# When ScalarE's evacuations, Silu and the stores of the gated product are issued in a hybrid block's gate/up loop

## The chip, the core and the metric

The kernel runs on one core of a Trainium2 chip. The core has a matrix engine (TensorE, PE in the profile), three engines that work on tiles in on-chip memory (VectorE = DVE, ScalarE = ACT, GpSimd = POOL) and a queue engine that starts transfers (SyncE = SP). ScalarE and GpSimd start transfers too. The metric is device microseconds of one execution, as a median of several runs.

## The reference

One transformer block in float32: a sequence of 512 tokens, width 2048. The input projection feeds a state space mixer (SSD) and an attention with three branches; their results go through the output projection. Then follows a gated feed-forward part and a final norm. What the change touches is the feed-forward part:

```python
    v = rmsnorm(h, ffn_norm_w[l])
    h = h + (jax.nn.silu(v @ w_gate[l]) * (v @ w_up[l])) @ w_down[l]
return rmsnorm(h, final_norm_w)
```

Its width is 5632, so the gate and up products are [512 x 2048] by [2048 x 5632] each, and the down product is [512 x 5632] by [5632 x 2048].

## The kernel before

**Numbers.** Every float32 operand is split into a high part, rounded to the matrix engine's fp32r format, and a low part, the rest. A product is made of three matmuls (high by high, high by low, low by high). High parts are written by ScalarE (`a_hi`, line 122), low parts by VectorE (`lo`, line 125, and `neg_lo`, line 128).

**Strassen-like products.** In the feed-forward part a 2 x 2 block product is made with seven products M1 to M7 (names on line 44) of sums of blocks. For the activations these sums are made once, into seven tiles: V0, two tiles in U, and four tiles T. For the weights, four blocks and two sums per pair of column blocks are kept: "11", "12", "22", "S1", "S3" (and "21" in the down part); S1 and S3 come from two transfers, of which the second adds into the first. `quad` (line 1290) says which block each product takes, and which sums have to be made by VectorE just before (for M6 and M3).

**Gate/up.** The 5632 columns are 22 pairs `u` of 256. A pair has two sides, 0 for gate and 1 for up. For pairs 1 to 20 side 0 runs all seven products in the order `SEQ` (M1 M5 M6 M2 M7 M3 M4, line 46), and then side 1 does. The first pair (0) and the last (21) run their sides side by side (`both_sides`, line 1484, with an explicit order). One product is one *step* (`run_step`, line 1156): 8 groups of two matmuls, one with 512 columns (high weights by high and low activations together), one with 256. Each side has three PSUM banks (`BANK`, line 59): M1, M6, M7 and M4 add up in bank X, M5 and M3 in bank R, and M2 is added in bank W to a copy of M1. Adding up in the bank saves additions later, but each partial sum has to be read out before the next product adds to it.

**What follows a product.** `gu_after` (line 1363) reads each bank out after its product: M1 is copied by ScalarE from bank X to bank W (line 1379), M6 is copied from X (line 1381), M2 from W (line 1389), M5 from R (1395), M7 and M3 are added by VectorE, M4 is copied (1411) and then VectorE adds halves of all four buffers into the side's result. After M4 of the gate side VectorE multiplies by the row scale (`rr`), ScalarE applies Silu in two instructions (1417 and 1418), and VectorE multiplies by the row scale again (`times_r`, 1426). After M4 of the up side VectorE multiplies both sides, and `g_forms` (1430) splits the result and four sums of its quarters into high and low parts, and stores them in DRAM (`g_d`, line 1450, issued on ScalarE's queue).

**Order of issue.** From `run_rest` on, the program order of each engine's queue is the order in which the Python code issues. Each step first issues the weight forms of later steps (`prep`: the high part of the step three ahead, with the sums, and the low part of the step two ahead), then its matmuls, and after each of its 8 matmul groups a *tick* (`Sched`, line 71). A generator that yields n goes on n ticks later, so 8 ticks are one step. After the matmuls the step issues its read-out. An engine does its instructions in its own program order, so what is issued first can hold up what stands behind it.

**Down.** 35 visits (`VISITS`, line 23) each multiply some rows of weight blocks for one of 8 column blocks `j`. The hidden activations come back from DRAM into a ring of 7 slots (`GRING`), which are the seven activation tiles of the gate/up part: a slot can be loaded when the last pair's product that reads the tile is done. `feed` (line 1529) is called before each step and issues these loads on ScalarE's queue, in two halves: products 0 to 3 of the list (M1, M2, M3, M6) in the first half, and M5, M7, M4 in the second. In a visit the order is `SEQ_D` (M1 M2 M6 M3 M7 M4 M5), so that the fifth product is the first to read a second half. `place` (line 1068) picks room for a weight block on its way in: for the down part in a zone of 38 rows, first at multiples of six, then anywhere. `advance` (1084) issues a load as soon as there is room, on SyncE's queue, and an adding transfer on GpSimd's.

**Waits between transfers.** Transfers issued by SyncE and ScalarE share a rotation of eight completion semaphores, so that a new one can wait for the one eight before it.

Of the kernel before, what the change touches and what calls it, by code (L numbers as in the profile page):

```python
# [10 lines left out]
AF = mybir.ActivationFunctionType  # L11
# [6 lines left out]
NP = NFF // 2  # L18
# [7 lines left out]
GRING = 7  # L26
# [17 lines left out]
M1, M2, M3, M4, M5, M6, M7 = range(1, 8)  # L44
# [10 lines left out]
NA, NZ, NZ2 = 76, 48, 38  # L55

NR, NE = 48, 8
# [55 lines left out]
def body(ctx, tc, xT, w_in, w_out, w_gate, w_up, w_down, w1k, w1v, cols, rows, kst, out):  # L113
    nc = tc.nc
    act, dve, pool, pe = nc.scalar, nc.vector, nc.gpsimd, nc.tensor
    sch = Sched()
# [4 lines left out]
    def a_hi(dst, src, scale=1.0):  # L121
        act.activation(dst, src, AF.Copy, scale=scale)  # L122
# [7 lines left out]
    def mul(eng, o, a, b):  # L130
        eng.tensor_tensor(o, a, b, ALU.mult)  # L131

    def add(eng, o, a, b):
        eng.tensor_tensor(o, a, b, ALU.add)  # L134
# [825 lines left out]
    P2 = {}  # L960
# [96 lines left out]
    def take(n, *found):  # L1057
        found = [x for x in found if x]
        if not found:
            return None  # L1060
        _, at, z = min(found, key=lambda x: x[0])
        z.busy[at:at + n] = [True] * n
        return z, at


    fz, az, tz, hz, ez = Zone("Z", NZ), Zone("A", 8), Zone("A2", 6), Zone("R", NR), Zone("E", NE)

    def place(b):
        n = b.n
        if b.down:  # L1070
            return take(n, fz.find(n, NZ2, range(0, NZ2 - 5, 6)) or fz.find(n, NZ2), ez.find(n) if "E2" in P2 and n <= NE else None,
                        tz.find(n) if "A2" in P2 and n <= 6 else None)
        return take(n, fz.find(n), az.find(n))

# [288 lines left out]
    def gu_after(u, side, got):  # L1363
        both = u in (0, NP - 1)

        def after(pr):
            def ev(p):
                wv = P2["A"][:, 12:28, :].rearrange("p (b a) t -> p b (a t)", b=4)
                if both:
                    wv = wv[:, 2 * side:2 * side + 2]  # L1370
                u2, m5 = wv[:, 0 if both else 1, :], wv[:, 1 if both else 3, :]
                ct = P2["CT"].rearrange("p (s c a) t -> p s c (a t)", s=2, c=2)
                c = ct[:, side].rearrange("p a t -> p (a t)")
                g = ct[:, 0].rearrange("p a t -> p (a t)")
                c4 = c.rearrange("p (a t) -> p a t", a=4)
                if pr == M1:
                    if u:
                        got["W"] = bank()
                    act.activation(got["W"] if u else m5, p, AF.Copy)  # L1379
                elif pr == M6:  # L1380
                    act.activation(u2, p, AF.Copy)
                elif pr == M2:
                    if u == 0:
                        add(dve, m5, p, m5)
                        add(dve, c4[:, 0], m5[:, lo_h], m5[:, hi_h])
                    elif both:
                        fold(c4[:, 0], p)
                    else:
                        act.activation(wv[:, 0, :], p, AF.Copy)
                elif pr == M5:  # L1390
                    if u == 0:
                        dve.tensor_tensor(m5, p, m5, ALU.subtract)
                        add(dve, u2, p, u2)
                    else:
                        act.activation(m5, p, AF.Copy)
                elif pr == M7:
                    add(dve, m5, p, m5)
                    if u == 0:
                        add(dve, c4[:, 1:4:2], wv[:, :, lo_h], wv[:, :, hi_h])
                elif pr == M3:  # L1400
                    if u == 0:
                        act.activation(m5, p, AF.Copy)
                    else:
                        add(dve, u2, p, u2)
                        if both:
                            add(dve, c4[:, 1:4:2], wv[:, :, lo_h], wv[:, :, hi_h])
                elif pr == M4:
                    if both:
                        fold(c4[:, 2], p)
                    else:  # L1410
                        act.activation(wv[:, 2, :], p, AF.Copy)
                        add(dve, c4, wv[:, :, lo_h], wv[:, :, hi_h])
                    if side == 0:
                        rr = rrow[:, None, :].to_broadcast([128, 2, 512])
                        c2 = ct[:, 0]
                        mul(dve, c2, c2, rr)
                        act.activation(g[:, 0:512], g[:, 0:512], AF.Silu)
                        act.activation(g[:, 512:1024], g[:, 512:1024], AF.Silu, scale=-1.0)
                        sch.add(times_r(c2, rr))
                    else:  # L1420
                        mul(dve, c, c, g)
                        sch.add(g_forms(u))
            return ev
        return after

    def times_r(c2, rr):
        yield 8
        mul(dve, c2, c2, rr)

    def g_forms(u):  # L1430

        ct = P2["CT"].rearrange("p (s c a) t -> p s c (a t)", s=2, c=2)
        g = ct[:, 1]
        tg = ct[:, 0].rearrange("p a t -> p (a t)").rearrange("p (a t) -> p a t", a=4)
        sg = P2["ST"][:, 0:14, :].bitcast(F32R).rearrange("p (v s) t -> p v s t", s=2)
        a_hi(sg[:, 0, 0, :], g[:, 0, lo_h])
        a_hi(sg[:, 1:3, 0, :], g[:, 1, :].rearrange("p (a t) -> p a t", a=2), scale=-1.0)
        gq = g.rearrange("p c (a t) -> p (c a) t", a=2)
        dve.tensor_tensor(tg[:, 1, :], gq[:, 1, :], gq[:, 0, :], ALU.subtract)
        add(dve, tg[:, 2, :], gq[:, 1, :], gq[:, 3, :])  # L1440
        add(dve, tg[:, 0, :], tg[:, 1, :], gq[:, 3, :])
        dve.tensor_tensor(tg[:, 3, :], tg[:, 0, :], gq[:, 2, :], ALU.subtract)
        yield 4
        lo(dve, sg[:, 0, 1, :], g[:, 0, lo_h], sg[:, 0, 0, :])
        neg_lo(sg[:, 1:3, 1, :], g[:, 1, :].rearrange("p (a t) -> p a t", a=2), sg[:, 1:3, 0, :])
        a_hi(sg[:, 3:7, 0, :], tg)
        yield 4
        lo(dve, sg[:, 3:7, 1, :], tg, sg[:, 3:7, 0, :])
        yield 6
        nc.scalar.dma_start(g_d[u].rearrange("v p n -> p v n"), f(sg).rearrange("p v s t -> p v (s t)"))  # L1450
        sch.flags.add(("g", u))
# [32 lines left out]
    def both_sides(u, order, seq):  # L1484
        loads.extend(qs[u, int(a[0])][a[1:]] for a in order.split())
        bk = {i: gu_banks() for i in range(2)}
        af = {i: gu_after(u, i, bk[i][0]) for i in range(2)}
        for n, (side, p) in enumerate(seq):
            ev = af[side](p)
            if u == 0 and n in (1, 4):  # L1490
                ev = step_r3(ev)
            q = qs[u, side]
            b, sums = q["form"][p]
            if u == 0 and p in (M3, M6):
                sums = [(q["11"], q["S1"]), (q["12"], q["11"])] if p == M3 else ()
            if u and n == 0:
                before = lambda: P2.update(spare=P2["ST"][:, 14:16, :])
            else:
                before = start_ff(n) if u == 0 and n < 7 else None
            s = Step(b, v_rhs(p), bk[side][1](p), after=ev, before=before, sums=sums,  # L1500
                     wide=True)
            if (u, side) == (NP - 1, 1):
                n = V_SLOT.index(V_OF[p]) - GRING
                done[n, 0] = done[n, 1] = s.i

    done = {}
    both_sides(0, "011 111 0S1 012 112 1S1 0S3 022 1S3 122", [(i, p) for p in (M1, M2, M3) for i in range(2)] +
               [(0, M6), (0, M5), (0, M7), (1, M6), (0, M4), (1, M5), (1, M7), (1, M4)])
    for u in range(1, NP - 1):
        for side in range(2):  # L1510
            add_loads(qs[u, side])
# [15 lines left out]
    later = {}  # L1527

    def feed(i):

        for half, r in ((0, slice(0, 4)), (1, slice(4, 7))):
            n = nxt["ring", half]
            if n < NP and max(done.get((n - GRING, half), i), later.get(n, 0)) + 3 <= i:
                if n == NP - 1:
                    sch.run_until(("g", n))
                G[n] = P2["slot"][n % GRING]
                nc.scalar.dma_start(f(G[n][:, r]).rearrange("p v s t -> p v (s t)"),
                                    g_d[n, r].rearrange("v p n -> p v n"))
                nxt["ring", half] += 1
        if "H0" not in P2 and len(G) > 0 and not any(az.busy):  # L1540
            load_h(0)
            P2["H0"] = True
# [352 lines left out]
```

## Time and profile before

| | |
|---|---|
| median of 3 runs | 2302.05 us (2302.01 to 2304.55) |
| the profiled execution's own time | 2301.49 us |
| its span, first to last instruction | 2299.5 us |
| mean granted TensorE clock | 0.982 |
| busy TensorE / VectorE / ScalarE / GpSimd | 95% / 79% / 51% / 18% |
| mean transfer rate | 181 GB/s |
| input projection to output projection | 0 to 893 us |
| first gate/up pair | 893 to 944 us |
| pairs 1 to 20 | 944 to 1764 us |
| last pair | 1764 to 1807 us |
| down part and end | 1807 to 2299 us |

The profile is of one execution. In its timelines a row has the start, the length, the engine, the line, the operation, the tiles (written <- read), the shapes and how many such instructions were merged; in square brackets stands how long the engine had been idle before, and what ended that. In a list of waits stand the total, the number and the longest. A line such as 122 belongs to a helper, so that the tiles say which use it is.

### The profile page before, as it was taken

Reading aid. Unit: us, or ns where it says so; the run is one execution under the profiler, and the core shown is the slowest. Engines: PE = TensorE matmul, PEld = TensorE weight load, DVE = VectorE, ACT = ScalarE, POOL = GpSimd, SP = SyncE. Lnnn points to the kernel's source line nnn. Section 1 sums busy time; section 2 is a strip of 40 time slices with the busy share of each in tenths; the row PEclk is TensorE's granted clock in tenths of the full one; section 3 lists DMA queues with packets and bytes.
Section 4 is the critical chain, followed back from the end, with each engine's and each line's share of the span. In section 5 each row is a group of like instructions: output and inputs, shape, how many; then the busy total and the mean of one; then the engine's idle time right before and its main releaser. Section 6 shows DMA issues by size and latency. Waiting matters only on the chain. (4 is left out here: it accounts for less than half of the span.)

```text
span 2299.5 us, 34934 instructions
## 1 busy us (share of the span) xinstructions
PE 2184.9 (95%) x12904; PEld 1916.1 (83%) x12904; DVE 1824.0 (79%) x2858; ACT 1183.4 (51%) x1961; POOL 425.2 (18%) x433
## 2 busy tenths in 40 slices
PE   7999999999989899999999999999999898999996
PEld 5888888888868687888888888888888798999996
DVE  6699766688888667888788887888878787888897
ACT  4564456566766444555555555555555343333453
POOL 1011334323232133000001000000000121121222
PEclk8999999999989899999999999999999999999998
DMA  5222343122324265878777787787877969696974
GB/s 174 92 70 74 130 139 103 64 92 73 127 70 138 90 214 146 230 206 249 212 231 224 209 248 211 234 222 209 247 212 216 315 223 298 171 301 165 303 193 132
DMA packets 168554, 417.16 MB, mean 181 GB/s; under 512 B 16592, under 2 KB 23520, under 8 KB 168384
## 3 DMA queue, kind: packets, MB, share of 16 engines
q1 hardware_dynamic: 99776, 252.24, 32.4%
q0 software_dynamic: 25888, 76.72, 17.1%
q10 hardware_dynamic: 42720, 85.99, 11.0%
q8 instruction: 101, 1.65, 0.3%
q14 instruction: 69, 0.57, 0.1%
HBM read 353.80 MB, written 57.41 MB: 179 GB/s over the span
## 5 line engine op out<-in xcount | busy, mean ns | idle before, releaser
L122 ACT ACTIVATE R<-Z 128x1024 fp32r<-128x1024 f32 (+4 forms) x459 | 420.6, 931 | 448.5 <-DVE Z L134 316.5
L125 DVE TENSOR_TENSOR R<-Z,R 128x1024 fp32r<-128x1024 f32 (+4 forms) x365 | 387.2, 1067 | 42.2 <-ACT R L122 25.6
L232 PE MATMUL ps_g<-u,whi 128*128 128x512 f32 x720 | 285.5, 397 | 0.2 <-DVE h L131 0.2
L234 PE MATMUL ps_g<-u,wlo 128*128 128x512 f32 x720 | 284.0, 394 | 0.0
L233 PE MATMUL ps_g<-u,whi 128*128 128x512 f32 x720 | 283.4, 394 | 0.0
L1168 PE MATMUL ps_s<-u,R 128*128 128x512 f32 (+1 forms) x1152 | 251.4, 347 | 2.3 <-DVE R L125 2.3
L1168 PEld LDWEIGHTS ps_s<-u,R 128*128 128x128 f32 x1152 | 187.8, 188 | 29.7 <-DVE R L125 2.8
L125 DVE TENSOR_TENSOR wlo<-wraw,whi 128x512 fp32r<-128x512 f32 x196 | 151.4, 775 | 64.9 <-ACT whi L122 64.3
L122 ACT ACTIVATE whi<-wraw 128x512 fp32r<-128x512 f32 x196 | 122.6, 626 | 131.3 <-PE ps_g L233 84.7
L234 PEld LDWEIGHTS ps_g<-u,wlo 128*128 128x128 f32 x720 | 135.3, 188 | 26.9
L232 PEld LDWEIGHTS ps_g<-u,whi 128*128 128x128 f32 x720 | 135.4, 188 | 25.9 <-DVE h L131 0.5
L233 PEld LDWEIGHTS ps_g<-u,whi 128*128 128x128 f32 x720 | 135.5, 188 | 25.3
L1168 PE MATMUL ps_s<-T,R 128*128 128x512 f32 (+1 forms) x552 | 127.3, 357 | 27.2 <-ACT ps_t L1379 27.2
L1168 PE MATMUL ps_t<-u,R 128*128 128x512 f32 x592 | 134.0, 352 | 2.1 <-DVE A L134 2.1
L134 DVE TENSOR_TENSOR A<-ps_g,A 128x512 f32<-128x512 f32 (+1 forms) x114 | 74.0, 656 | 77.2 <-PE ps_g L1168 38.5
L1168 PE MATMUL ps_g<-u,R 128*128 128x512 f32 (+1 forms) x600 | 131.9, 348 | 1.4 <-DVE R L125 1.4
L1168 PEld LDWEIGHTS ps_s<-T,R 128*128 128x128 f32 x552 | 88.3, 188 | 52.1 <-ACT ps_t L1379 39.7
L1168 PE MATMUL ps_g<-T,R 128*128 128x512 f32 (+1 forms) x584 | 127.1, 349 | 1.3 <-DVE R L125 1.3
L122 ACT ACTIVATE R<-A 128x1024 fp32r<-128x1024 f32 (+3 forms) x78 | 73.3, 939 | 97.8 <-DVE A L134 60.6
L1168 PE MATMUL ps_s<-V,R 128*128 128x512 f32 (+1 forms) x568 | 122.8, 347 | 0.0
L125 DVE TENSOR_TENSOR E<-Z,R 128x1024 fp32r<-128x1024 f32 x94 | 114.7, 1221 | 9.6 <-PE ps_t L1168 5.6
L1172 PE MATMUL ps_g<-u,R 128*128 128x256 f32 (+1 forms) x353 | 114.9, 326 | 7.6 <-ACT R L122 7.6
(486 smaller groups left out, 5728.3 us busy)
## 6 DMA issues: line engine op xcount, KB each, us to landing
Z<-in_w_gate SPq DMA_DIRECT2D x96, 512.0 KB, 4.7
Z<-in_w_up SPq DMA_DIRECT2D x93, 512.0 KB, 6.2
wraw<-in_w_in SPq DMA_DIRECT2D x164, 256.0 KB, 2.6
g_d<-A ACTq DMA_DIRECT2D x22, 1792.0 KB, 7.5
Z<-in_w_gate POOLq DMA_DIRECT2D x39, 512.0 KB, 7.8
Z<-in_w_up POOLq DMA_DIRECT2D x37, 512.0 KB, 5.7
Z<-in_w_down SPq DMA_DIRECT2D x58, 320.0 KB, 5.8
Z<-in_w_down SPq DMA_DIRECT2D x39, 384.0 KB, 3.9
```

The costliest lines, as they stand in the source:

```text
L122: act.activation(dst, src, AF.Copy, scale=scale)
L125: eng.tensor_tensor(dst, src, f(hi), ALU.subtract)
L134: eng.tensor_tensor(o, a, b, ALU.add)
L232: pe.matmul(p, hi_t[i][:, j, :], ah, start=(k == 0), stop=False)
L233: pe.matmul(p, hi_t[i][:, j, :], al, start=False, stop=False)
L234: pe.matmul(p, lo_t[i][:, j, :], ah, start=False, stop=(k == u.nk - 1))
L1168: pe.matmul(o, w, x, start=start, stop=(k == n - 1 and o is q), skip_group_check=not fresh[0])
L1172: pe.matmul(q, h[:, k, :], ah, start=(k == 0), stop=False)
```

## The change

Five things change.

1. In `place`, a down weight block is put in the best free room anywhere in the zone; it is not first tried at multiples of six.
2. In the first pair, M1 is copied to the buffer `u2` in place of `m5`. M2 is no longer read out by itself; it stays in its bank until M6 is done, and is then added to M1. The order of the second half of the pair alternates the sides to the end: M6 M6 M5 M5 M7 M7 M4 M4. In the list of weight loads, the up side's S3 comes ahead of the gate side's 22.
3. Silu is no longer issued right behind M4 of the gate side. A generator issues it 10 ticks later in pairs 1 to 20 (in the second matmul group of the second step after M4), at once in the first and last pair; the second multiplication by the row scale follows 6 ticks behind it (before, 8 ticks behind M4). A flag makes M4 of the up side wait in the issuing program until that multiplication is issued.
4. `g_forms` starts 10 ticks later. With its further waits of 4, 4 and 6 ticks, the store to `g_d` is issued at tick 24 behind M4 of the up side; before, it was tick 14.
5. In `feed`, several loads can be issued in one step. The first halves of slots 0 and 1 wait for the product behind the one that frees them, and the second halves of slots 0 to 4 wait until the slot of the last first half is free.

```diff
@@ place
-            return take(n, fz.find(n, NZ2, range(0, NZ2 - 5, 6)) or fz.find(n, NZ2), ez.find(n) if "E2" in P2 and n <= NE else None,
+            return take(n, fz.find(n, NZ2), ez.find(n) if "E2" in P2 and n <= NE else None,
@@ gu_after
                 if pr == M1:
                     if u:
                         got["W"] = bank()
-                    act.activation(got["W"] if u else m5, p, AF.Copy)
+                    act.activation(got["W"] if u else u2, p, AF.Copy)
                 elif pr == M6:
+                    if u == 0:
+                        add(dve, u2, got["W"], u2)
+                        add(dve, c4[:, 0], u2[:, lo_h], u2[:, hi_h])
                     act.activation(u2, p, AF.Copy)
                 elif pr == M2:
-                    if u == 0:
-                        add(dve, m5, p, m5)
-                        add(dve, c4[:, 0], m5[:, lo_h], m5[:, hi_h])
-                    elif both:
+                    if u and both:
                         fold(c4[:, 0], p)
-                    else:
+                    elif u:
                         act.activation(wv[:, 0, :], p, AF.Copy)
...
                         mul(dve, c2, c2, rr)
-                        act.activation(g[:, 0:512], g[:, 0:512], AF.Silu)
-                        act.activation(g[:, 512:1024], g[:, 512:1024], AF.Silu, scale=-1.0)
-                        sch.add(times_r(c2, rr))
+                        sch.add(silu(u, g, c2, rr, 0 if both else 10))
                     else:
+                        sch.run_until(("r", u))
                         mul(dve, c, c, g)
                         sch.add(g_forms(u))
...
-    def times_r(c2, rr):
-        yield 8
+    def silu(u, g, c2, rr, n):
+        yield n
+        act.activation(g[:, 0:512], g[:, 0:512], AF.Silu)
+        act.activation(g[:, 512:1024], g[:, 512:1024], AF.Silu, scale=-1.0)
+        yield 6
         mul(dve, c2, c2, rr)
+        sch.flags.add(("r", u))
@@ g_forms
+        yield 10
         a_hi(sg[:, 0, 0, :], g[:, 0, lo_h])
@@ the first pair
-    both_sides(0, "011 111 0S1 012 112 1S1 0S3 022 1S3 122", [(i, p) for p in (M1, M2, M3) for i in range(2)] +
-               [(0, M6), (0, M5), (0, M7), (1, M6), (0, M4), (1, M5), (1, M7), (1, M4)])
+    both_sides(0, "011 111 0S1 012 112 1S1 0S3 1S3 022 122", [(i, p) for p in (M1, M2, M3) for i in range(2)] +
+               [(i, p) for p in (M6, M5, M7, M4) for i in range(2)])
@@ feed
-            n = nxt["ring", half]
-            if n < NP and max(done.get((n - GRING, half), i), later.get(n, 0)) + 3 <= i:
+            while nxt["ring", half] < NP:
+                n = nxt["ring", half]
+                at = max(done.get((n - GRING, half), i), later.get(n, 0))
+                if n < 2 and half == 0:
+                    at = done.get((n + 1 - GRING, 0), i)
+                if n < 5 and half == 1:
+                    at = done.get((4 - GRING, 0), i) + n // 2
+                if at + 3 > i:
+                    break
```

## The prediction

> **What bounds the kernel now.** I read the page first, then TensorE's waits, then windows, then the timelines of TensorE, ScalarE and VectorE around one pair of gate/up columns.
>
> ```profile
> PE 2184.9 (95%) x12904; PEld 1916.1 (83%) x12904; DVE 1824.0 (79%) x2858; ACT 1183.4 (51%) x1961; POOL 425.2 (18%) x433
> ...
> PE ps_s L1168 <- ACT ps_t L1379: 27.2, 39, 1.1
> ...
> PE ps_s L1172 <- DMA u<-g_d: 7.2, 2, 5.4
> PE ps_s L1172 <- ACT R L122: 5.8, 2, 5.0
> ```
>
> TensorE is busy 95% of the span, so only its gaps can be won. The largest group is 39 waits for line 1379, the copy of product M1 out of PSUM. Two waits are for the ring of hidden activations (u<-g_d), at the step from gate/up to down.
>
> ```profile
> 781.00:784.40 3.40, 1.86 (x14) 1.54 (x14) 3.40 (x11) 2.67 (x8) 0.49 (x1) 1.00 0.20 77
> ...
> 941.50:944.90 3.40, 3.40 (x12) 2.82 (x12) 1.55 (x2) 1.34 (x2) 0.85 (x1) 0.50 0.29 45
> 944.90:1763.60 818.70, 791.48 (x4480) 683.87 (x4479) 667.07 (x679) 443.07 (x580) 69.09 (x80) 1.00 0.80 225
> 1772.90:1818.10 45.20, 35.41 (x198) 30.58 (x199) 32.22 (x40) 20.81 (x31) 4.47 (x4) 0.93 1.02 363
> 1811.90:1818.70 6.80, 3.07 (x14) 3.07 (x15) 6.38 (x12) 4.14 (x7) 0.74 (x1) 0.50 1.02 373
> ```
>
> In each row stand the window, its length, busy PE, PEld, DVE, ACT, POOL, the granted clock, the DMA share and GB/s. The steady pairs (third row) run at full clock although TensorE pauses in each; VectorE is 81% busy there. The granted clock is halved in two of these windows, 941.5 and 1811.9.
>
> Now the steady pair. A step is one product, 16 matmuls; a side's order is M1 M5 M6 M2 M7 M3 M4.
>
> ```profile
> 964.14 2.94 PE L1168 MATMUL ps_s<-V,R 128*128 128x512 f32 x16
> 970.26 3.04 PE L1168 MATMUL ps_s<-T,R 128*128 128x512 f32 x16 [0.38 <-ACT ps_t L1379]
> 973.14 2.95 PE L1168 MATMUL ps_t<-u,R 128*128 128x512 f32 x16
> 981.52 2.94 PE L1168 MATMUL ps_s<-u,R 128*128 128x512 f32 x16
> 987.08 2.98 PE L1168 MATMUL ps_g<-T,R 128*128 128x512 f32 x16
> 991.12 3.09 PE L1168 MATMUL ps_s<-T,R 128*128 128x512 f32 x16 [1.06 <-ACT ps_t L1379]
> ```
>
> From 981.52 (M4, up side) to 987.08 (M5, next gate side) are two steps, 5.56 us: a step without a wait is 2.78. From 964.14 (M1, up side) to 970.26 (M6) are two steps in 6.12, 0.56 too long, and the following step has 2.88, 0.10 too long: gate to up costs 0.66. At the other boundary M5 to M6 takes 4.04, 1.26 too long, and about 0.15 after it: up to the next gate costs 1.41. With 20 boundaries of the first kind and 19 of the second that is 13.2 + 26.8 = 40.0 us of excess, the size of 39 waits plus their restarts. The cause stands on ScalarE:
>
> ```profile
> 967.61 0.64 ACT L1417 ACTIVATE A<-A 128x512 f32<-128x512 f32 x1 [2.55 <-DVE A L131]
> ...
> 969.63 0.58 ACT L1379 ACTIVATE ps_t<-ps_s 128x512 f32<-128x512 f32 x1
> ...
> 987.75 0.94 ACT L122 ACTIVATE A<-A 128x256 fp32r<-128x256 f32 x2 [2.55 <-DVE A L131]
> 988.60 1.05 ACT L122 ACTIVATE R<-Z 128x1024 fp32r<-128x1024 f32 x1
> ...
> 990.50 0.57 ACT L1379 ACTIVATE ps_t<-ps_s 128x512 f32<-128x512 f32 x1
> ...
> 992.55 0.37 ACTq L1450 DMA_DIRECT2D g_d<-A  x1
> ...
> 995.92 0.58 ACT L1381 ACTIVATE A<-ps_s 128x512 f32<-128x512 f32 x1
> ```
>
> The Silu (967.61) and the result splits (987.75) are each 2.55 us late for VectorE's product, and the M1 copy stands behind them in ScalarE's program order. M6 adds into the bank that the copy reads, so it waits.
>
> **The change part by part.** (a) Silu behind the next M1's copy. Its two instructions now follow ten ticks, in the second matmul group of M5. M1 ends at 964.14 + 2.78 = 966.92, and the copy can end 0.6 later, near 967.6, 2 us before M6 (969.70). Then come one weight copy (1.05) and the two Silu (0.6 each): about 969.9. Behind Silu now stand the M5 copy, whose bank is next written by M3, three steps on, and, on VectorE, the second product with the scale (1.22), moved to the end of M5: 971.2. It has behind it the sum for M3's weights (1.15: 972.4), this the weight copy of ScalarE (1.05: 973.4), and this the evacuation of M6 (0.58: 974.1), which M7 needs at 964.14 + 4 x 2.78 = 975.26. About 1.2 us are left, so this boundary loses its wait: 20 x 0.66 = **13.2 us gained**. If the spare were used up the wait would only move; gaining nothing is the low bound.
>
> (b) Result splits ten ticks later. This also frees the M1 copy, but what the splits start has to be followed to its end: their sums and low parts on VectorE, then at tick 24 the store of g_d, issued **on ScalarE's queue** (L1450). Before, tick 14 put that issue ahead of the M5 copy, where lateness was harmless. Tick 24 is the last tick of M6, so it now stands directly ahead of the M6 copy (L1381), and M7 adds into that bank. The issue waits for the last low part on VectorE. That chain, from the second boundary's rows:
>
> ```profile
> 986.49 1.22 DVE L131 TENSOR_TENSOR A<-A 128x1024 f32<-128x1024 f32 x1
> 987.75 0.43 DVE L1439 TENSOR_TENSOR A<-A 128x256 f32<-128x256 f32 x1
> ...
> 989.22 1.22 DVE L125 TENSOR_TENSOR R<-Z,R 128x1024 fp32r<-128x1024 f32 x1
> 990.36 0.42 DVE L125 TENSOR_TENSOR A<-A 128x256 fp32r<-128x256 f32 x1
> ...
> 991.30 1.22 DVE L125 TENSOR_TENSOR A<-A 128x1024 fp32r<-128x1024 f32 x1
> ...
> 993.68 1.23 DVE L134 TENSOR_TENSOR Z<-Z 128x1024 f32<-128x1024 f32 x1
> 994.83 1.22 DVE L125 TENSOR_TENSOR R<-A,R 128x1024 fp32r<-128x1024 f32 x1
> ```
>
> Start to start, a low part of weights takes 1.14 (989.22 to 990.36), the four sums 1.47 (987.75 to 989.22), the two small low parts 0.94 (990.36 to 991.30), a weight sum 1.15 (993.68 to 994.83). In the new order VectorE does after the product (done 987.71): low part of M6's weights, of M2's, the four sums, the two small low parts, the sum for M3, the low part of M7's weights, then the last low part. 987.75 + 1.14 + 1.14 + 1.47 + 0.94 + 1.15 + 1.14 = 994.73, and the last one ends 1.22 later at 995.95. The issue takes 0.37, the M6 copy 0.58, with some 0.12 between them for semaphores (an estimate: M1's copy ends at 991.07 and M6 starts at 991.12, 0.05 for one hand-over): M7 could start near 997.0. Undisturbed it would start at 987.08 + 3 x 2.78 = 995.42. So the wait goes from M6 to M7 and is 1.6 us, with 0.13 for the restart 1.73, against 1.41 before: 19 x 0.32 = **6.1 us lost**. Bounds: no wait at all, 26.8 gained; VectorE 0.3 later, 11.8 lost. I take the walk, since each of its durations is a row of this stage.
>
> (c) First pair side by side to its end; M1's copy into the other half of the buffer.
>
> ```profile
> 898.35 0.60 ACT L1379 ACTIVATE A<-ps_s 128x512 f32<-128x512 f32 x1 [2.17 <-POOL A L1249]
> ...
> 904.82 2.83 PE L1168 MATMUL ps_s<-u,R 128*128 128x256 f32 x15 [2.33 <-DVE R L125]
> ...
> 939.37 0.68 DVE L134 TENSOR_TENSOR A<-ps_t,A 128x512 f32<-128x512 f32 x1
> ...
> 940.20 0.47 PE L1168 MATMUL ps_t<-u,R 128*128 128x512 f32 x1 [2.06 <-DVE A L134]
> ```
>
> The first M1 copy waited 2.17 us for a GpSimd operation that reads the buffer it writes; the half it now writes is last read earlier. The VectorE chain behind it, which ends in the wait of 2.33, moves up: 2.2 us (bounds 0 and 4). The wait at 940.20 is M4 of the up side right behind M7 of the same side, with the bank still read at 939.37; side by side, M4 of the gate side (2.78 us) lies between, and the add ends 1.9 us after M7. That saves 2.06, and 1.7 for the 3.4 us of half clock in the window at 941.5. Against it, pair 0's store meets pair 1 as in (b), with a shorter VectorE chain (0.42 in place of 1.22): about 0.8. Sum **5.2**, bounds 0 and 7. The moved M2 evacuation and the loads' order cost nothing: each of these steps brings VectorE one low part (1.14) and at most 1.2 us of evacuation in 2.78 us of matmuls; without that cover the M2 evacuations (two of 1.1) would come back.
>
> (d) Ring loads: first halves early, second halves held back, and a looser placement of down weights.
>
> ```profile
> 1774.04 2.86 PE L1168 MATMUL ps_g<-T,R 128*128 128x256 f32 x15 [1.30 <-DVE R L125]
> ...
> 1792.51 2.84 PE L1168 MATMUL ps_g<-u,R 128*128 128x256 f32 x15 [1.41 <-DVE R L125]
> ...
> 1809.62 0.39 PE L1172 MATMUL ps_s<-u,R 128*128 128x256 f32 x1 [1.85 <-DMA u<-g_d]
> ...
> 1815.63 0.58 PE L1172 MATMUL ps_s<-u,R 128*128 128x256 f32 x1 [5.40 <-DMA u<-g_d]
> ...
> 1823.83 0.29 PE L1172 MATMUL ps_g<-u,R 128*128 128x256 f32 x1
> ...
> 1824.55 0.28 PE L1172 MATMUL ps_s<-V,R 128*128 128x256 f32 x1
> ```
>
> These four gaps make 10.0 us, and the 6.8 us at half clock add 3.4: 13.4 is the most to win. But the bytes stay: 45.2 us at 363 GB/s and a full DMA share. The second boundary's M1 starts at 987.08 - 2.78 = 984.30, and 19 pairs of 14 x 2.78 + 0.66 + 1.41 = 41.0 later, near 1763, the last pair. The last first half had landed at 1815.63, its second half (0.79 MB, 2.2 us at this rate) near 1817.8: 55 us after that start. The new loads begin later, and all of them cannot be there before about 56. The first product that reads second halves is the visit's fifth; at 0.12 us a matmul (1823.83 to 1824.55 for six) and 15 a product it would stand at 14 x 2.78 + 4 x 1.8 = 46.1. So the wait moves from the first product to the fifth, which ends near 57 instead of near 63 (1824.55 + 1.8): 6 won, less about 2 for a half clock after it. **4 us**, bounds 0 and 13.4. The placement I cost at nothing: the one long wait of the down stage had a cause in DMA,
>
> ```profile
> 1948.79 0.74 ACT L122 ACTIVATE R<-Z 128x640 fp32r<-128x640 f32 x1 [8.10 <-DMA Z<-in_w_down]
> ```
>
> and more room does not move bytes faster; bounds plus and minus 8 (its 5.0, and 3 for the clock).
>
> **Sum.** 13.2 - 6.1 + 5.2 + 4 = 16.3. The profiled execution took 2301.5 (span 2299.5); the median of the runs is 0.6 above it. 2302.05 - 16.3 = **2285.7 us**.
>
> **The rivals.** *No new wait at M7*: if the issue did not hold up the M6 copy, 26.8 + 6.1 = 32.9 more are won: 2253. Against it: 987.75 and 990.50 show that ScalarE keeps its program order where what is ahead waits for VectorE. *Half clock at every boundary*, the case on the slower side: the moved gap is 1.4 us (a delay of 1.26 showed as 1.06 of idleness). In the window at 781 TensorE idled 1.54 of 3.4 us and the clock was then halved; at 1.30 and 1.41 above it was not. If the clock is set over stretches of 3.4 us, as halves of 3.4 and 6.8 us suggest, a gap 0.15 us longer than mine would lie whole in one stretch at about 60% of 19 boundaries, at 1.7 each: 19 + 3 = 22, so 2308; if all do, 32 + 3, so 2321. Between 1.41 and 1.54 it decides. The Trainium skill (TensorE: Matmul & The Clock Gate, "Why this matters for your kernels") speaks of gaps over about 3 us, by which the 1.4 would be harmless and the sum stays; the same page's "A second HAM failure mode: psum-queue depth-cycling" has frequent short pauses halve the clock, which the 39 gaps at clock 1.00 here do not bear out. *The moved copy is not early after all* (weight copies of ScalarE ahead of it wait too): (a) and (b) give nothing, and 5.2 + 4 less a few for the first pair leaves 2297 to 2302.
>
> **How the numbers follow.** The forecast has 0.62, no new wait 0.13, the half clock 0.10, no early copy 0.08; 0.07 lies between. The range 2264 to 2303 holds the forecast with half of (b)'s upper bound, the no-copy case and part of the clock case. A difference under 0.2% (4.6 us) cannot be told from none here. Faster: 0.62 + 0.13 + 0.07 = 0.82; same 0.10; slower 0.08.
>
> **What would show it.** Right: no waits for L1379; some 19 waits of M7 for L1381 of about 1.4 us, each behind L1450; a DMA wait in the fifth product of the down stage; no gap near 940. Wrong: M7 without a wait, granted clock below 1.00 in the steady pairs, or new waits of M6 for VectorE.

## The result, and the profile after

The changed kernel takes **2276.16 us** as a median (2275.06 to 2277.89); the kernel before took 2302.40 beside it. The ratio is 0.9885, with an interval of 0.9868 to 0.9902: 26 us faster, where 16.3 were forecast. The profiled execution took 2275.06, its span is 2273.3. Medians and intervals in this document leave out slow executions, such as one of x12's four, 4313 us long.

The page of the changed kernel, its engines:

```profile
PE 2177.7 (96%) x12904; PEld 1916.4 (84%) x12904; DVE 1822.6 (80%) x2858; ACT 1187.4 (52%) x1961; POOL 426.1 (19%) x433
```

TensorE is busy for 7 us less than before (2184.9), so most of the gain is idleness that went away. The waits of TensorE in the changed kernel (total, number, longest):

```profile
PE ps_s L1168 <- ACT A L1384: 26.3, 20, 2.4
...
PE ps_s L1172 <- DMA u<-g_d: 2.9, 1, 2.9
...
PE ps_g L1172 <- DMA u<-g_d: 1.8, 1, 1.8
...
PE ps_s L1172 <- ACT R L122: 0.3, 1, 0.3
```

The 39 waits for the M1 copy (line 1379) are gone. In their place stand 20 for the M6 copy, now line 1384, and they add up to almost as much: 26.3 us against 27.2. The waits for the ring and for weight copies on these lines of the down part fell from 7.2 + 5.8 to 5.0. Windows of the changed kernel, the steady pairs first, then three in the down part (columns as in the prediction):

```profile
944.90:1763.60 818.70, 792.39 (x4511) 688.96 (x4510) 666.16 (x689) 449.15 (x583) 69.98 (x81) 1.00 0.80 226
...
1874.00:1899.00 25.00, 25.00 (x214) 25.00 (x213) 20.34 (x31) 10.39 (x17) 4.88 (x4) 1.00 0.68 197
1899.40:1920.20 20.80, 20.50 (x171) 20.09 (x170) 17.74 (x28) 7.56 (x13) 4.05 (x4) 1.00 1.05 381
1920.20:1933.90 13.70, 13.10 (x107) 12.59 (x106) 11.30 (x17) 4.74 (x7) 2.98 (x3) 1.00 1.05 372
```

The granted clock stays at 1.00 in the steady pairs, and in the eleventh visit of the down part (last row), which before took 22.1 us at 0.85.

One pair boundary of the changed kernel, in the timelines of TensorE, ScalarE and VectorE:

```profile
1143.80 2.94 PE L1168 MATMUL ps_s<-V,R 128*128 128x512 f32 x16
...
1152.17 2.94 PE L1168 MATMUL ps_t<-u,R 128*128 128x512 f32 x16
1156.39 0.51 PE L1168 MATMUL ps_s<-u,R 128*128 128x512 f32 x1 [1.28 <-ACT A L1384]
...
1167.65 2.98 PE L1168 MATMUL ps_g<-T,R 128*128 128x512 f32 x16
1170.47 2.99 PE L1168 MATMUL ps_s<-T,R 128*128 128x512 f32 x16
...
1146.78 0.58 ACT L1379 ACTIVATE ps_t<-ps_s 128x512 f32<-128x512 f32 x1 [1.12 <-PE ps_s L1168]
...
1155.33 0.37 ACTq L1454 DMA_DIRECT2D g_d<-A  x1
1155.74 0.60 ACT L1384 ACTIVATE A<-ps_s 128x512 f32<-128x512 f32 x1 [1.55 <-DVE A L125]
...
1146.00 1.23 DVE L131 TENSOR_TENSOR A<-A 128x1024 f32<-128x1024 f32 x1
...
1154.09 1.22 DVE L125 TENSOR_TENSOR A<-A 128x1024 fp32r<-128x1024 f32 x1
```

The M1 copy runs at 1146.78, as soon as M1 is done. VectorE's last low part ends at 1155.31; 0.02 later the store's issue (1454) starts, behind it the M6 copy, and M7 starts at 1156.39. From M2 (1152.17) to M7 are 4.22 us instead of 2.78. At the other boundary M5 (1167.65) to M6 (1170.47) are 2.82: no wait.

### The profile page after: what moved, and what is told of

Same layout as the page of the kernel before. It is cut to its first block, busy times and chain, and to the rows that moved or that the text cites. A ratio compares the mean times of both kernels' runs of the same rounds, so it can differ in the third digit from the quotient of the medians.

```text
span 2273.3 us, 35008 instructions
## 1 busy us (share of the span) xinstructions
PE 2177.7 (96%) x12904; PEld 1916.4 (84%) x12904; DVE 1822.6 (80%) x2858; ACT 1187.4 (52%) x1961; POOL 426.1 (19%) x433
## 5 line engine op out<-in xcount | busy, mean ns | idle before, releaser
L125 DVE TENSOR_TENSOR R<-Z,R 128x1024 fp32r<-128x1024 f32 (+4 forms) x363 | 393.6, 1092 | 41.1 <-ACT R L122 30.5
L1168 PE MATMUL ps_s<-u,R 128*128 128x512 f32 (+1 forms) x1152 | 253.4, 349 | 26.8 <-ACT A L1384 26.3
L1168 PEld LDWEIGHTS ps_s<-u,R 128*128 128x128 f32 x1152 | 186.6, 188 | 60.0 <-ACT A L1384 32.9
L134 DVE TENSOR_TENSOR A<-ps_g,A 128x512 f32<-128x512 f32 (+1 forms) x114 | 73.9, 655 | 73.1 <-PE ps_g L1168 39.1
L1172 PE MATMUL ps_g<-u,R 128*128 128x256 f32 (+1 forms) x353 | 115.1, 326 | 9.0 <-ACT R L122 7.1
L1173 PE MATMUL ps_g<-u,R 128*128 128x256 f32 (+1 forms) x353 | 114.1, 323 | 0.0
```

What stands on the lines that cost most here:

```text
L125: eng.tensor_tensor(dst, src, f(hi), ALU.subtract)
L1168: pe.matmul(o, w, x, start=start, stop=(k == n - 1 and o is q), skip_group_check=not fresh[0])
L1172: pe.matmul(q, h[:, k, :], ah, start=(k == 0), stop=False)
L1173: pe.matmul(q, h[:, k, :], al, start=False, stop=False)
```

## The experiments

Each stage is timed from the trace by the first matmul of its first product. The stage ahead of gate/up is the same code in all, yet ends between 889 and 895, so stages tell more than medians do. But the stages are those of one execution, the profiled one, and executions of one kernel differ by 3 us and more: the profiled one of x3 is the fastest of its four (2278.3), that of x7 the slowest of four (2280.9), that of x5 the slowest of five (2294.5). Pairs 2 to 20 are 19 equal pairs. All in us:

| kernel | gate/up starts | pair 0 | pair 1 | pairs 2-20 | pair 21 | down, end | median | ratio, interval |
|---|---|---|---|---|---|---|---|---|
| before | 892.8 | 51.6 | 39.9 | 779.3 | 43.0 | 492.9 | 2302.4 | |
| changed | 893.0 | 46.2 | 41.7 | 771.9 | 39.2 | 481.3 | 2276.2 | 0.9885, 0.9868-0.9902 |
| x1: store a tick later | 894.9 | 46.0 | 40.3 | 750.5 | 39.2 | 479.2 | 2251.5 | 0.9782, 0.9762-0.9803 |
| x2: store on SyncE | 891.3 | 44.7 | 39.9 | 746.4 | 39.2 | 481.7 | 2247.1 | 0.9758, 0.9739-0.9777 |
| x3: old placement | 891.6 | 47.1 | 43.3 | 771.8 | 39.2 | 483.6 | 2281.6 | 0.9914, 0.9893-0.9935 |
| x5: Silu alone | 892.5 | 51.6 | 39.4 | 768.3 | 42.3 | 498.6 | 2290.0 | 0.9947, 0.9930-0.9964 |
| x6: splits alone | 893.1 | 51.6 | 40.2 | 782.8 | 44.6 | 493.3 | 2307.1 | 1.0021, 1.0011-1.0030 |
| x7: old ring order | 892.5 | 44.7 | 44.2 | 771.6 | 41.0 | 484.5 | 2278.4 | 0.9891, 0.9876-0.9906 |
| x9: first pair alone | 893.0 | 46.2 | 43.7 | 779.0 | 43.1 | 485.8 | 2293.3 | 0.9957, 0.9940-0.9974 |
| x10: ring order alone | 889.7 | 51.6 | 39.9 | 779.0 | 41.0 | 487.8 | 2292.4 | 0.9951, 0.9936-0.9966 |
| x11: ring on GpSimd | 891.0 | 52.2 | 39.9 | 779.6 | 43.0 | 501.8 | 2309.3 | 1.0043, 1.0028-1.0059 |
| x12: x2, ring on GpSimd | 889.2 | 46.0 | 39.9 | 746.7 | 39.2 | 495.4 | 2259.7 | 0.9830, 0.9800-0.9861 |
| x13: longer gap | 893.5 | 46.2 | 42.3 | 784.5 | 39.2 | 481.9 | 2288.2 | 0.9938, 0.9920-0.9957 |

x5, x6, x9, x10 and x11 start from the kernel before, the others from the changed one. There is no run of the placement alone: without the first pair's new order of loads one down block finds no six adjacent free rows in its zone.

### Is it the store's issue that holds up the M6 copy?

Theory: ScalarE's queue stands at the store's issue until VectorE is done, and the copy of M6 stands behind it. Rival: the copy is late for other work of ScalarE. Two ways to free it: the issue one tick later, so that it falls behind the copy, or on SyncE's queue.

```diff
 # x1, in g_forms
-        yield 6
+        yield 7
 # x2, in g_forms
-        nc.scalar.dma_start(g_d[u]...
+        nc.sync.dma_start(g_d[u]...
```

> The changed kernel with one edit: the store of the gated product is issued at tick 25 in place of 24, that is behind the copy of M6. Theory (the issue on ScalarE's queue holds up the M6 copy): the 20 waits of M7 for L1384 (26.3 us, with restarts 31) go, and 2276 becomes 2245 +- 5. Rival (VectorE's chain itself makes the M6 copy late, through the weight sum and the weight copy ahead of it): at most 3 us less, 2273 to 2276. Second rival (the block moves on to the M2 copy and a later product waits): 2260 to 2276, with new waits in the steady pairs.

> The changed kernel with the store of the gated product issued on SyncE's queue, at tick 24 as before. Theory (only the place of the issue on ScalarE's queue matters): the waits of M7 go as with tick 25, 2245 +- 6; SyncE then waits up to 3 us for the last low part, and weight loads behind it come later, which has spare time in the steady pairs. Rival (transfers or VectorE make M7 late): 2272 to 2276. If the loads behind the store become late: new waits for weights, 2250 to 2265.

TensorE's waits for the M6 copy in x1:

```profile
PE ps_s L1168 <- ACT A L1384: 5.9, 7, 1.4
```

and in x2:

```profile
PE ps_s L1168 <- ACT A L1384: 2.7, 4, 1.0
```

Pairs 2 to 20 are 21.4 us shorter in x1 and 25.5 in x2; what is left in x2, 746.4 / 19 = 39.3 a pair, is close to 14 x 2.78 = 38.9. The theory holds: one DMA issue, 0.37 us long, cost the changed kernel 25 us by its place. Pair 1 is back at 39.9 in x2, too, from 41.7. x2 is the best kernel of this study, 55 us under the one before.

x1's 2251.5 lies 1.5 above its range. Of its seven waits, six stand at the other boundary, from gate to up, with no store near. One of them, in ScalarE's and TensorE's rows:

```profile
1245.22 1.07 ACT L122 ACTIVATE R<-Z 128x1024 fp32r<-128x1024 f32 x1 [3.00 <-DMA Z<-in_w_up]
...
1250.78 0.58 ACT L1384 ACTIVATE A<-ps_s 128x512 f32<-128x512 f32 x1
...
1251.41 1.89 PE L1168 MATMUL ps_s<-u,R 128*128 128x512 f32 x9 [1.41 <-ACT A L1384]
```

ScalarE stood 3.00 us for a load of up weights, and Silu, the second product with the row scale and the copy of M6 came late behind it. Three of the four waits in x2 are of this kind. So with the store out of the way a load of weights is what such a pair waits for next; no experiment changes that.

### The two moves alone

x5 takes `silu` into the kernel before, x6 only the line `yield 10` at the head of `g_forms`.

> The kernel before with Silu alone moved behind the copy of the next M1 (10 ticks in pairs 1 to 20). Theory by the prediction's term (a): the 20 waits at the boundary from gate to up go, 19 or 20 waits of about 1.06 stay, 2302.4 - 13.2 = 2289 +- 2. Rival (the M1 copy stays late behind other work, or a wait takes its place at M7): 2298 to 2303.

> The kernel before with the result splits ten ticks later, and nothing else. By the prediction's term (b): the 19 waits of M6 at the step from up to gate go, 19 waits of M7 behind the store's issue take their place and cost 0.32 more each, 2302.4 + 6 = 2308. By what the traces of the changed kernel and of Silu alone leave for it (7.4 less 11.0 over pairs 2 to 20, so 3.6 lost, and some 2 in pair 1): 2306, plus or minus 3. Rival (the store's issue doesn't hold up the copy of M6, and the moved splits free M6): 2302 - 27 = 2275. The 20 waits from gate to up, about 0.4 us each, stay in every case.

TensorE's waits within the steady pairs, x5:

```profile
PE ps_s L1168 <- ACT ps_t L1379: 20.7, 19, 1.4
```

and x6:

```profile
PE ps_s L1168 <- ACT A L1381: 23.9, 19, 1.6
PE ps_s L1168 <- ACT ps_t L1379: 6.7, 20, 0.4
```

Both times lie in the range forecast for them. Silu alone takes the 20 waits at gate to up away and leaves the 19 at up to gate; pairs 2 to 20 gain 11.0 (the down part, which the edit does not touch, starts earlier and takes 5.7 longer; part of that may be this execution's own, which is 4.5 above its kernel's median, and the cause is open). The splits alone turn those 19 into waits of M7 and lose 3.5. The sum, 7.5, is what pairs 2 to 20 of the changed kernel gained (7.4). So the moved splits were a loss in this form, and worth having only once the store's issue no longer stands ahead of the copy of M6, as in x1 and x2.

### What won the down part

The changed kernel gained 3.7 us in pair 21 and 11.6 behind it, where the prediction had 4 for the ring and nothing for the placement. 8.3 of the 11.6 lie in one visit, the eleventh. First the placement and the ring's order were undone, then the ring's order and the first pair's order were changed alone.

```diff
 # x3: the changed kernel
+            return take(n, fz.find(n, NZ2, range(0, NZ2 - 5, 6)) or fz.find(n, NZ2), ...
 # x7: the changed kernel with feed() of before; x10: before with the new feed()
 # x9: before with gu_after and both_sides(0, ...) of the change
```

> The changed kernel with the old placement of down weights (multiples of six first). Theory (the looser placement let weight loads start earlier, and so won the 8.3 us wait of the eleventh visit and small ones behind it): 2276 + 8 to 11 = 2284 to 2287, and the eleventh visit takes 20 us or more again. Rival (the order of the ring's loads, or the earlier arrival at the down part, won it): 2275 to 2278, the eleventh visit stays under 15 us.

> The changed kernel with the ring's loads as they were before (one half at a time, each as soon as its slot is free); placement, first pair, Silu and splits as changed. Open is what won 11.6 us behind the last pair, 8.3 of them in one down visit (the tenth after the first, 22.0 us before, 13.8 after), since the old placement brought back only about 2.5. Theory (the order of the ring's loads won it: the transfers queued behind them come earlier): the last pair takes about 42 us in place of 39.2, the down part about 490 in place of 481, that visit about 22 again; the time is 2276 + 3 + 9 = 2288, plus or minus 4. Rival (placement and the first pair's order of loads, which shift every later load, won it): last pair 42, down part 482 to 484, that visit about 14; 2278 to 2281.

> The kernel before with the changed order of the ring's loads alone. Theory (the order of the ring's loads won the down part): last pair 39.2 us in place of 42.95, the long visit about 14 us in place of 22; 2302.4 - 3.7 - 8.3 = 2290, plus or minus 4. By the prediction's term (d), which put the ring at 4 and the long wait of the down part at nothing: 2298. Rival (the long visit goes with placement and the first pair's loads): 2298 to 2300, with the visit still at 22.

> The kernel before with the changed first pair alone (order of products, M1's copy into the other buffer, its own order of loads). By the prediction's term (c) without the store that meets pair 1: 6.0 won, first pair and pair 1 together 85.5 us in place of 91.5; 2302.4 - 6.0 = 2296. The order of the first pair's loads shifts later weight loads too; if that bears on the down part, its 492.9 us move by several us, and the long visit of 22 us with them (2288 if that goes). Rival (the gaps only move to other products): 2300 to 2302.

Pair 21 and what follows, together, gain 7.0 in x10 (1.9 + 5.1) and 6.9 in x9, in both against the kernel before; against the changed kernel they lose 2.3 with the old placement (x3) and 5.0 with the old ring order (x7). The last two go by executions at opposite ends of their kernels; by the medians the old placement costs 5.4 and the old ring order 2.2. So each part has a share, but how the placement and the ring's order compare is not settled, and no single one carries the visit: with the old ring order the eleventh visit takes 14.1, with the old placement 15.7, with the first pair alone 16.7, with the ring alone 12.4 after 4.0 more in the visit before it.

Of the forecasts, x3's 2281.6 lies between theory and rival. x7 by itself looks like its rival (2278.4, the visit at 14.1), yet x10 shows that the ring's order alone takes the long wait out of that visit, so neither theory of the expectations of x7 stands. x10's 2292.4 lies in its range, but its last pair took 41.0 where 39.2 was forecast. x9's 2293.3 is near its 2296 by luck: pairs 0 and 1 gained 1.6, not 6.0, since 3.8 were lost again in pair 1 (its M6 waits 2.17 us for the copy of M1, and half clock follows), and the rest came from the down part.

The kernel before loses the most of all here. Its windows: 25 us ahead, the ninth and tenth visits, the eleventh:

```profile
1890.00:1915.00 25.00, 24.48 (x207) 24.28 (x206) 21.29 (x30) 10.02 (x16) 5.28 (x5) 1.00 0.71 210
1915.80:1935.70 19.90, 19.90 (x170) 19.90 (x169) 17.45 (x28) 7.68 (x13) 2.56 (x3) 1.00 0.99 346
1935.70:1957.80 22.10, 16.07 (x108) 15.14 (x107) 11.79 (x18) 5.37 (x8) 3.27 (x3) 0.85 0.91 305
```

Against the last two rows of the changed kernel's windows above: before, 19.9 x 346 + 22.1 x 305 = 13.6 MB in 42.0 us, 324 GB/s; after, 20.8 x 381 + 13.7 x 372 = 13.0 MB in 34.5 us, 377 GB/s. Without a wait the three visits take 32.3 (9.96 + 9.96 + 12.41, the shortest times of such visits). The two rates are means. The same stretch of the kernel before, cut where its transfers change:

```profile
1915.80:1921.80 6.00, 6.00 (x53) 6.00 (x52) 5.48 (x10) 2.57 (x5) 0.99 (x2) 1.00 0.86 252
1921.80:1947.80 26.00, 21.81 (x179) 21.18 (x178) 17.55 (x27) 6.49 (x11) 3.83 (x3) 1.00 1.05 378
1947.80:1951.80 4.00, 2.16 (x8) 1.86 (x9) 2.24 (x4) 3.01 (x5) 1.01 (x2) 0.58 0.51 155
1951.80:1957.80 6.00, 6.00 (x40) 6.00 (x39) 3.96 (x6) 0.99 (x2) 0.00 (x0) 0.71 0.91 283
```

and of the changed kernel, from 6 us ahead of its ninth visit:

```profile
1893.40:1899.40 6.00, 6.00 (x53) 6.00 (x52) 3.63 (x6) 0.64 (x1) 0.00 (x0) 1.00 1.01 308
1899.40:1933.40 34.00, 33.10 (x271) 32.18 (x270) 28.64 (x43) 12.30 (x20) 6.76 (x6) 1.00 1.05 377
```

With a full share (1.05) both kernels move the same 377 or 378 GB/s. What differs is when the transfers fill up: after, from 6 us ahead of the ninth visit on; before, from 6 us into it (0.86 until then), and they stand half idle again (0.51) for the 4 us around TensorE's long wait. So for 26 us this stretch is set by transfers, and the gain shows as transfers that fill up earlier, not as a higher rate. What held them back before could be read from SyncE's queue, which issues the weights. Its waits, kernel before, 1880 to 1960:

```profile
SPq L1107 <- DVE R L125: 41.5, 21, 7.6
SPq L1107 <- DMA T<-g_d: 12.7, 3, 6.0
...
SPq L1107 <- DMA V<-g_d: 5.2, 1, 5.2
SPq L1107 <- DMA u<-g_d: 1.2, 1, 1.2
```

Weight loads stood 12.7 + 5.2 + 1.2 = 19.1 us for ring loads, which they do not read: the rotation of completion semaphores. In the trace the first part of the late block is issued at 1933.31, right behind the landing of a ring load at 1933.24. x11 takes the later ring loads out of that rotation, x12 does so in the best kernel.

```diff
-                nc.scalar.dma_start(f(G[n][:, r])...
+                (nc.scalar if n < GRING else nc.gpsimd).dma_start(f(G[n][:, r])...
```

> The kernel before, with the ring's loads from the eighth slot use on (n of 7 and more) issued on GpSimd's queue, which has completion semaphores of its own; the same bytes, in the same steps. Theory (the long visit's late weight load is held up by the rotation: SyncE's issue of its first part at 1933.31 stood until a ring load issued eight transfers before had landed at 1933.24): without ring loads in the rotation the weight loads go out as their room comes free, and the visit of 22.0 us takes about 14; 2302.4 - 8 = 2294, plus or minus 4. Rival (bytes: the transfers share the same engines, so whichever goes first, that weight load lands as late): the visit stays at 20 to 22, 2300 to 2304. Rival on the other side (GpSimd's queue: each issue takes 0.9 us there in place of 0.4 and stands ahead of the adding transfers): the visit over 23, 2305 and more.

> The changed kernel with the store of the gated product on SyncE's queue (2247.07 by itself) and the ring's loads from the eighth on on GpSimd's queue. The long visit takes 13.8 us of 12.4 at least there, so by the rotation theory 1 to 3 are left to win: 2245, plus or minus 3. By the rival that GpSimd's queue delays the adding transfers: 2250 and more. By the rival of bytes: 2247.

SyncE's waits in x11, 1880 to 1960:

```profile
SPq L1107 <- DVE R L125: 62.6, 28, 12.2
```

and rows of its TensorE and GpSimd timelines:

```profile
1937.05 0.58 PE L1172 MATMUL ps_g<-V,R 128*128 128x256 f32 x1 [3.59 <-DMA V<-g_d]
...
1912.80 1.29 POOL L134 TENSOR_TENSOR Z<-Z 128x512 f32<-128x512 f32 x1 [7.37 <-DMA Z<-in_w_down]
...
1915.75 1.11 POOL L1537 DMA_DIRECT2D V<-g_d  x1
```

The waits for ring loads are gone from SyncE's queue, and the eleventh visit takes 12.7, as the theory has it. Its time fails: the wait moves one visit ahead to a ring load, so that the three visits take 39.1 us where the theory had 34, SyncE now waits longer for room (62.6 against 41.5), and later visits lose 11 us against the kernel before. Both kernels with the ring on GpSimd are slower, by 8 and by 13 us, as the rival on GpSimd's side has it, but the rows show another reason than the rival gave: the ring loads of this stretch are issued from 1915.75 on, behind an addition of GpSimd that stood 7.37 us for a weight load, where the kernel before issued the first at 1908.90. Here the issue stands behind a wait of its queue, where the store's issue on ScalarE makes others wait.

So x11 changes two things at once and can't tell what the rotation cost by itself. What is shown is that this stretch is bound by transfers for most of its length and that other orders of issue have its three visits 3 to 8 us shorter than the kernel before; how much of that the rotation, the placement and the ring's order each held back stays **open**.

### How long may a gap be before the clock halves?

The prediction's rival on the slower side put the bound between 1.41 and 1.54 us of idleness. x13 makes the 20 gaps longer by a copy on ScalarE behind the store's issue; it works on a buffer that is dead by then.

```diff
         nc.scalar.dma_start(g_d[u]...
+        act.activation(tg[:, 0:2, :], tg[:, 0:2, :], AF.Copy)
```

> The changed kernel with one more copy on ScalarE (512 columns, about 0.6 us, of a buffer that is dead by then, onto itself) directly behind the store's issue, ahead of the copy of M6. The gap before M7 grows from about 1.25 to 1.85 us in each of 20 pairs. It asks whether the half clock waits just beyond the gaps that the change left. By the prediction's rival (a stretch of 3.4 us that holds over 1.54 us of idleness is followed by one at half clock): a gap of 1.85 lies so in some 65% of 20 cases, 1.7 us each, 22 us: 2276 + 12 + 22 = 2310, with granted clock 0.50 in a dozen stretches among the steady pairs. By a bound near 3 us, as the Trainium skill has it (TensorE: Matmul & The Clock Gate, "Why this matters for your kernels"): 2276 + 12 = 2288 and clock 1.00 throughout the pairs.

Windows of x13, each one stretch of 3.41 us of the clock's own grid:

```profile
952.20:955.61 3.41, 1.66 (x9) 1.47 (x10) 1.98 (x3) 2.83 (x5) 0.86 (x1) 1.00 0.85 250
1034.12:1037.53 3.41, 1.60 (x9) 1.21 (x8) 2.00 (x3) 2.54 (x5) 0.86 (x1) 1.00 0.93 267
1037.53:1040.94 3.41, 3.41 (x12) 2.91 (x11) 1.17 (x2) 1.35 (x3) 0.00 (x0) 0.50 1.02 360
1406.17:1409.58 3.41, 1.66 (x9) 1.49 (x10) 2.00 (x3) 2.83 (x5) 0.86 (x1) 1.00 0.86 249
1447.13:1450.54 3.41, 1.61 (x9) 1.26 (x9) 2.00 (x3) 2.60 (x5) 0.86 (x1) 1.00 0.86 283
1450.54:1453.96 3.42, 3.42 (x13) 2.94 (x12) 1.25 (x2) 1.43 (x2) 0.00 (x0) 0.50 1.01 352
```

The gaps are 1.70 to 1.81 us long (one 2.90), and two of the 20 are followed by a stretch at half clock: those where a stretch holds 3.41 - 1.60 = 1.81 and 3.41 - 1.61 = 1.80 us of idleness. Stretches with 1.75 (952.20 and 1406.17) are not followed by one. The time is 2288.2, so the rival is far off, and the mechanism that it names is there all the same, with its bound 0.25 us higher than I read. The other forecast has the time, 2288, but not its condition: the clock was not 1.00 throughout.

The other traces bear the bound out. Two stretches, of x2 and of x11:

```profile
1772.93:1776.34 3.41, 1.60 (x14) 1.40 (x13) 3.38 (x6) 1.19 (x2) 1.30 (x2) 1.00 1.05 392
902.03:905.45 3.42, 1.64 (x10) 1.46 (x11) 2.33 (x6) 2.50 (x3) 1.35 (x2) 1.00 0.24 93
```

The first holds 1.81 us of idleness and is followed by half clock, the second 1.78 and is not. From the start of gate/up to the last visit, the thirteen traces have 48 stretches of the grid at full clock with 1.80 us or more of idleness, and every one is followed by half clock; none with 1.78 or less is. (The last visit of the kernel is left out: there one stretch of x7 with 1.84 is not followed by half clock, and the reason is not known.)

## Why the prediction was right or wrong

**(a), Silu behind the next M1 copy: right, a little large.** Forecast 0.66 a boundary, 12.5 over pairs 2 to 20; Silu alone (x5) brought 11.0, or 0.58 each, and left no wait at gate to up. The rival "the moved copy is not early" is out: the M1 copy starts at 1146.78, 0.2 us after its product.

**(b), the splits: the walk was right almost to the tenth.** It put M7 at 997.0 for an M1 at 984.30, so 12.7 behind it; the row has 1156.39 - 1143.80 = 12.59. The order on VectorE and ScalarE is the one walked, the store's issue is what M7 waits for. With 14 x 2.78 = 38.9 a pair, the changed kernel's 771.9 / 19 = 40.6 leaves 1.7 of excess, against 1.73 forecast; that they agree so well is partly chance, since x2 without the wait still has 0.4 of excess. The price was too high: the splits alone (x6) lost 3.5 over pairs 2 to 20 where 6.1 was forecast. As (a) came out 1.5 too large and this loss 2.6 too large, the two errors nearly cancel in the sum: 12.5 - 6.1 = 6.4 forecast for these pairs, 7.4 measured. The rival "no new wait at M7" is what x1 and x2 make of the kernel, once the issue is elsewhere; it put 32.9 on it, and pairs 1 to 20 of x2 gained 25.5 + 1.8 = 27.3.

**(c), the first pair: pair 0 right, pair 1 mis-sized.** Pair 0 gained 5.4 of 2.2 + 3.8 = 6.0. For the store that meets pair 1 the prediction took 0.8, "with a shorter VectorE chain"; pair 1 got 1.8 longer (Silu alone makes it 0.5 shorter, so the store cost 2.3). Pair 1 of the changed kernel, TensorE and VectorE:

```profile
939.20 2.94 PE L1168 MATMUL ps_s<-V,R 128*128 128x512 f32 x16
...
952.91 3.04 PE L1168 MATMUL ps_s<-u,R 128*128 128x512 f32 x16 [2.38 <-ACT A L1384]
...
937.50 1.23 DVE L131 TENSOR_TENSOR A<-A,rrow 128x1024 f32<-128x1024 f32 x1
...
940.91 1.21 DVE L131 TENSOR_TENSOR A<-A,rrow 128x1024 f32<-128x1024 f32 x1
942.05 0.41 DVE L134 TENSOR_TENSOR A<-ps_t,A 128x256 f32<-128x256 f32 x1
942.50 1.23 DVE L131 TENSOR_TENSOR A<-A 128x1024 f32<-128x1024 f32 x1
```

The chain isn't shorter but later: with both M4 side by side, the gate side's two scale products (937.50 and 940.91) stand on VectorE in the same 5 us, and the product of the sides starts 3.30 behind M1, in a steady pair 2.20 (1146.00 - 1143.80). The gap is longer by the same 1.10: 2.38 against 1.28. So (c) came to 3.6 (5.4 - 1.8). Both numbers have luck in them. In x3 and x7 the same gap (2.39 and 2.41) lies in one stretch of the clock's grid, half clock follows, and pair 1 takes 43.3 and 44.2 in place of 41.7. And x2's pair 0 is 1.5 shorter than the changed kernel's because a gap of 3.1 us that both kernels have (it ends at 907.68 and at 909.35) is split by the grid in x2; in the changed kernel the clock is halved behind it, from 910.50 to 913.91.

**(d), ring and placement: the wrong term.** Forecast 4 and 0; it came to 15.4 (3.7 in pair 21, 11.6 behind it). In the first visit the forecast of the wait was met, that of its price was not: the fifth product waits 1.80 us for the ring, but the first one still waits 2.93, and half clock follows twice. The first visit takes 23.9 us in place of 21.5, so that pair 21 and this visit together gained 1.3, not 4. The step that failed is "more room does not move bytes faster", by which I priced the later visits at nothing. It is true of transfers at their full rate, 378 GB/s before and 377 after. But it was applied to a stretch that also holds 10 us at 252 and 155 GB/s, and there another order of issue does move the end. The two bounds together (13.4 and 8) hold the 15.4, but the terms behind them do not: the ring's order and the first pair's loads, each alone, brought 7.0 and 6.9 from pair 21 on, mostly in later visits, and the placement's share lies between 2.3 (stages) and 5.4 (medians). The whole is 26 us because (d) was 11.4 larger and (c) 1.6 smaller. The range 2264 to 2303 held the result by room that was left for (b), while the surplus came from (d): that part was luck.

**The half clock.** No gap of 1.2 to 1.6 us in the steady pairs was followed by a slower clock. The step that failed there is the bound of 1.54, taken from a window at 781 us: another stage, with matmuls of other shapes. Why the bound is lower there is not shown.

## What to carry to other kernels

A DMA issue takes its place in an engine's program order like any other instruction: one that waits for another engine belongs on a queue whose next instruction nobody waits for, or behind what is waited for, and 0.37 us in the wrong place cost 25 here. Moving work "later" needs a walk of each queue that it passes, and that walk, made from rows of the profile, can be good to 0.1 us. A mean rate over a stretch can hide pieces in which transfers stand still: 324 against 377 GB/s turned out to be the same 378 with 10 us of slack around it. Cut the stretch as finely as the wait is long before a change to the order of its loads is priced at nothing.

## What was not expected of the hardware

In the gate/up stage of x13 a stretch of 3.41 us with 1.75 us of idleness left the clock alone, one with 1.80 or 1.81 halved it for the next 3.41. The two half-clock stretches of x13 start 1450.54 - 1037.53 = 413.01 us apart, 121 times 3.413, so the grid runs on by itself, and a gap is split by it: the gap of 2.90 us that ends at 953.96 lies 1.14 in one stretch and 1.76 in the next, and costs no clock. The Trainium skill (TensorE: Matmul & The Clock Gate, "Why this matters for your kernels") names gaps over about 3 us; here a gap of 1.81 was enough where the grid held it whole.
